# Two scratch tiles instead of four for the decay operands of the chunked DeltaNet branch

## The chip, the cores and the metric

The kernel runs on one core of a Trainium2 chip. A core has five engines with a queue of instructions each: TensorE (PE in the profile) multiplies matrices into PSUM, VectorE (DVE) and ScalarE (ACT) work elementwise, GpSimd (POOL) does small elementwise work here, and SyncE (SP) issues most of the DMAs. An engine takes its instructions strictly in the order of its queue; an instruction that has to wait for another engine, or for a DMA, holds up all that stand behind it. The metric is the time of one execution on the device in microseconds, as the median of several runs.

## The reference

One decoder layer: a half-step SwiGLU, a mixing part, another half-step SwiGLU and a final norm, over 1024 tokens and 16 meta tokens, all in float32. The mixing part has two branches, (A) a chunked gated DeltaNet with 8 heads and (B) an RWKV-7 time mixing, which are gated and added. The change lies in branch A, in these lines of the reference:

```python
g = jnp.cumsum(g, axis=-1)
kb = k * beta[..., None]
diff = g[..., :, None] - g[..., None, :]
decay = jnp.where(incl, jnp.exp(jnp.where(incl, diff, 0.0)), 0.0)
m = jnp.where(strict, jnp.einsum('bhncd,bhnsd->bhncs', kb, k) * decay, 0.0)
tinv = lax.linalg.triangular_solve(m + eye, ...)
...
attn = jnp.einsum('bhncd,bhnsd->bhncs', q, k) * decay
qg = q * jnp.exp(g)[..., None]
k_tail = k * jnp.exp(g_last[..., None] - g)[..., None]
```

So each chunk needs a decay matrix, that matrix times beta (for the matrix that is inverted), `exp(g)` along the chunk, and the decay to the chunk's end.

## The kernel before

The program has three parts: `ffn1`, `middle`, `ffn2`. Both SwiGLU parts are long runs of large matmuls. `middle` goes over two segments of the sequence (first 528 columns with the meta tokens, then 512) and, in each, over 8 heads of A with a pair of heads of B: 16 iterations in all. The iterations are pipelined by hand in `schedule()`: a regular iteration runs `merge_blocks transitions operands+ inverses+ chains gates finish new_b++ new_a++`, where a plus means the next iteration's work, and two the one after. In words:

- `new_b` and `new_a` project the normalised input (three projections each, line 262 through `proj`), with the short convolution of A at lines 1168 to 1181: `xr` holds a projection, `acc` its convolved sum over the taps (L1173), `sg` the sigmoid (L932 to L934).
- `operands` makes what the recurrences need. For A it loads the cumulated gate of one head to all partitions (`gp`, L1232), subtracts the token's own value under a mask (`E`, L1236, four chunks), takes `exp` of that (L1238) and of `gp` (`eg`, L1239), makes the tail decay `kts` (L1240, L1241), copies the chunk ends of `eg` (`egl`, L1243 on POOL), and multiplies `E` by minus beta into `E2` (L1244 on POOL). Then PE makes the products of keys with keys and queries, two chunks to a PSUM bank (`gra`, L1252), and DVE turns each bank into `UA` (times `E2`, L1255) and `attn` (times `E`, L1256). `eg` is used last, at L1314.
- `inverse_inputs` and `inverses` send the diagonal blocks of `UA` and of B's matrices (`LT`) through DRAM (`scr`) into `Ub`, and invert them by 31 steps on DVE (L1364, L1366). `merge_blocks` (PE, L1399 and after) assembles the inverses.
- `transitions` (PE, L1056: `xp`, `vp`, `mp`, `np`; DVE: `mt` L1472, `AR` L1475, `vbk` L1478) and `chains` (PE, L1526 to L1550) run the recurrences; `gates` loads a small weight (`ugr`, L1561, turned into `ug` on ACT and DVE) and makes three projections; `finish` merges.
- `new_b` begins with another small load (`upr`, L1074), turned into `upz` (L1076 on ACT, L1078 on DVE).

Scratch of one kind of size comes from one pool tag, `tmp`, with `NTMP = 8` buffers (`tmp_tile`, L847). A new tile of that tag gets a buffer when an earlier tile has had its last reader; the first writer of the new tile waits for that reader. Of these tiles `new_b` takes 13 in each iteration, `new_a` 9, `operands` 4 (`eg`, `E`, `E2`, `gp`), `gates` one (`ugr`), and `segment`, between the two segments, takes one for `urs` and eight for `uh`.

Weights are loaded on SP by `fetchw` (L223) into one of two buffers `wraw` and split by ACT and DVE (L159, L160) into two halves of `w`, one weight ahead of its use; there are two buffers of `w`.

The order of each engine's queue is fixed when the program is built: the framework takes, for each engine, the instruction that stands first in the program among those that are ready by its own estimate of times. So a tile that gets its buffer earlier by that estimate can also move its first writer to an earlier place in a queue.

Of the kernel before, what the change touches and what calls it, by code (L numbers as in the profile page):

```python
# [11 lines left out]
ALU = mybir.AluOpType  # L12

P = 128
# [12 lines left out]
FULL = 512  # L27
CB = 64
NCB = FULL // CB
CA = 128  # L30
NCA = FULL // CA
# [815 lines left out]
def tmp_tile(g, name, w=528):  # L847
    return g.st.tile([P, w], F32, name=name, tag="tmp", bufs=NTMP)


def ch3(ap, c):
    return ap.rearrange("p (a b) -> p a b", b=c)
# [341 lines left out]
def operands(g, q):  # L1194

    nc, st, V, c, j, n, off = g.nc, g.st, g.V, q.c, q.j, q.n, q.off
    meta = q.s == 0
    fs = slice(off, off + FULL)
    tmp = lambda name, w=528: tmp_tile(g, name, w)
# [16 lines left out]
    if meta:  # L1216
# [3 lines left out]
        for h in range(2):  # L1220
# [3 lines left out]
                                op=ALU.mult)  # L1224


    eg = tmp("eg")[:, :FULL]
    E = ch3(tmp("E", 512), CA)
    E2 = ch3(tmp("E2", 512), CA)
    kts = st.tile([P, NCA], F32, name="kts", tag="kts")  # L1230
    gp = tmp("gp", FULL)
    nc.sync.dma_start(gp, g.gdr[q.s][j].unsqueeze(0).to_broadcast([P, FULL]))  # L1232
    gpv = ch3(gp, CA)
    gcol = c.tk[:, :, 8 + j : 9 + j]
    for i in range(NCA):
        nc.vector.scalar_tensor_tensor(E[:, i, :], gpv[:, i, :], c.tk[:, i, 8 + j : 9 + j], g.C("mA"),  # L1236
                                       op0=ALU.subtract, op1=ALU.min)
    nc.scalar.activation(E, E, AF.Exp)  # L1238
    nc.scalar.activation(eg, gp, AF.Exp)  # L1239
    nc.vector.tensor_tensor(kts.unsqueeze(2), gpv[:, :, CA - 1 : CA], gcol, op=ALU.subtract)  # L1240
    nc.scalar.activation(kts, kts, AF.Exp)  # L1241
    egl = q.egl = st.tile([P, NCA], F32, name="egl", tag="egl", bufs=2)
    nc.gpsimd.tensor_copy(egl.unsqueeze(2), ch3(eg, CA)[:, :, CA - 1 : CA])  # L1243
    nc.gpsimd.tensor_tensor(E2, E, c.tk[:, :, 16 + j : 17 + j].to_broadcast([P, NCA, CA]), op=ALU.mult)  # L1244
    attn = q.attn = st.tile([P, NCA, CA], F32, name="attn", tag="attn", bufs=2)
    UA = q.UA = st.tile([P, NCA, CA], F32, name="UA", tag="UA", bufs=1)
    for b in range(2):
        ps = g.mx.tile([P, 512], F32, name="gra", tag="mx")
        for c2 in range(2):
            i = 2 * b + c2  # L1250
            tsl = slice(off + i * CA, off + (i + 1) * CA)
            nc.tensor.matmul(ps[:, c2 * 256 : c2 * 256 + 256], lhsT=kq[:, 0, tsl], rhs=kq[:, :, tsl],  # L1252
                             start=True, stop=True)
        pv = ps.rearrange("p (c k t) -> p c k t", c=2, k=2)
        nc.vector.tensor_tensor(UA[:, 2 * b : 2 * b + 2, :], pv[:, :, 0, :], E2[:, 2 * b : 2 * b + 2, :], op=ALU.mult)  # L1255
        nc.vector.tensor_tensor(attn[:, 2 * b : 2 * b + 2, :], pv[:, :, 1, :], E[:, 2 * b : 2 * b + 2, :], op=ALU.mult)  # L1256
    if meta:
        gm = g.mx.tile([P, 512], F32, name="gm", tag="mx")
# [326 lines left out]
def finish(g, q):  # L1585
# [17 lines left out]
    else:  # L1603
        g.mg.append(u_tile(g, yb))


ACTIONS = {"new_a": new_a, "operands": operands, "inverses": inverses, "merge_blocks": merge_blocks, "transitions": transitions,
           "chains": chains,
           "gates": gates, "finish": finish, "fill": fill}
# [86 lines left out]
```

## Time and profile before

| what | value |
|---|---|
| runs | 3085.6, 3089.95 and 3088.84 us, median 3088.84 |
| the profiled execution's own time | 3085.29 us |
| its span, first to last instruction | 3083.5 us |
| mean granted TensorE clock | 0.989 |
| PE busy over the span | 2959.3 us (96%) |
| DVE busy | 1976.2 us (64%) |
| ACT busy | 1376.7 us (45%) |
| POOL busy | 354.9 us (12%) |

The profile is one execution with a time for each instruction. In its views, `out<-in` names the tile that is written and those that are read, `x4` the number of instructions in a row, and a bracket at the end of a row tells how long the engine was idle before it and whose end released it. PE's rows are pipelined and their ends modelled, and a few records can be missing, so PE's idle time is read from its waits rather than from 100% minus its share. Buffer numbers are left out of tile names, so `E2` stands there as `E`.

### The profile page before, as it was taken

To read this page: it belongs to the slowest core of one execution; us is meant where nothing else is said; L and a number is where in the kernel's file an instruction comes from. 1 tells how busy PE (TensorE), PEld (TensorE's weight loads), DVE (VectorE), ACT (ScalarE), POOL (GpSimd) and SP (SyncE) were. 2 spreads that over 40 slices of the span, in tenths; PEclk is the share of its full clock that TensorE was granted. 3 is DMA by queue.
4 is the path that set the end of the run, shared out by engine and by line. 5 is a ranking of instruction groups with operands and counts; after the bars stand their busy time and mean duration, and the time that the engine had idled before them with its cause. 6 is when DMAs were issued, how large, how long until landed. Compare 5 with 4: busy or idle time off the path is not lost.

```text
span 3083.5 us, 61656 instructions
## 1 busy us (share of the span) xinstructions
PE 2959.3 (96%) x25498; PEld 2539.0 (82%) x25498; DVE 1976.2 (64%) x3840; ACT 1376.7 (45%) x2404; POOL 354.9 (12%) x519
## 2 busy tenths in 40 slices
PE   8999999999899999999999999999999999999998
PEld 8999998998778888788777777777777888887886
DVE  6455454346677777787867877777866655555335
ACT  5322222126555656566566655665644432222114
POOL 0222220000001000001001000010100022222000
PEclk9999999999899999999999999999999999999999
DMA  3232224234222322333332332223354232224223
GB/s 125 82 97 83 83 86 158 79 101 140 62 74 73 79 70 59 85 79 75 97 89 73 84 81 75 75 75 84 109 148 165 68 104 94 83 83 170 86 78 114
DMA packets 257593, 287.19 MB, mean 93 GB/s; under 512 B 169296, under 2 KB 175440, under 8 KB 257312
## 3 DMA queue, kind: packets, MB, share of 16 engines
q1 hardware_dynamic: 253072, 271.43, 29.4%
q0 software_dynamic: 2512, 8.65, 0.7%
q8 instruction: 201, 3.29, 0.4%
q10 hardware_dynamic: 1728, 3.16, 0.3%
q14 instruction: 80, 0.66, 0.1%
HBM read 232.70 MB, written 50.47 MB: 92 GB/s over the span
## 4 chain that ended last, share of the span: by engine, by line
PE 54%; DVE 11%; ACT 7%; issue 2%; DMA 2%; SPq 0%; DVEq 0%; POOL 0%; ACTq 0%
PE pp L262 18%; PE pg L450 12%; PE pd L262 7%; PE pwo L262 3%; DVE w L160 1%; PE pg L474 1%; PE b L1542 1%; PE cs L1003 1%; PE gra L1252 1%; DMA ugr<-in_upg 1%; PE bkt L1281 1%; DVE tb L1364 1%; DVE mt L1472 1%; DVE Xb L1366 1%; PE vp L1056 1%
## 5 line engine op out<-in xcount | busy, mean ns | idle before, releaser
L262 PE MATMUL pp<-uk,w 128*128 128x512 f32 (+2 forms) x4824 | 975.1, 347 | 15.8 <-DVE w L160 9.3
L262 PEld LDWEIGHTS pp<-uk,w 128*128 128x128 f32 x4824 | 744.7, 191 | 109.1 <-DVE w L160 13.0
L159 ACT ACTIVATE w<-wraw 128x1024 fp32r<-128x1024 f32 (+2 forms) x330 | 326.3, 989 | 712.6 <-PE pd L262 287.6
L262 PE MATMUL pd<-hd,w 128*128 128x512 f32 (+2 forms) x2640 | 495.6, 349 | 11.3 <-DVE w L160 6.7
L262 PEld LDWEIGHTS pd<-hd,w 128*128 128x128 f32 x2640 | 427.5, 189 | 78.2 <-DVE w L160 8.6
L160 DVE TENSOR_TENSOR w<-wraw,w 128x1024 fp32r<-128x1024 f32 (+2 forms) x330 | 376.1, 1140 | 90.9 <-ACT w L159 85.7
L456 DVE TENSOR_TENSOR c<-c,pg 128x520 f32<-128x520 f32 (+1 forms) x280 | 189.2, 689 | 337.3 <-PE pg L450 278.3
L450 PE MATMUL pg<-bt,w 128*128 128x256 f32 (+2 forms) x2520 | 403.9, 317 | 0.0
L450 PEld LDWEIGHTS pg<-bt,w 128*128 128x128 f32 x2520 | 361.0, 188 | 32.9 <-DVE w L160 0.2
L450 PE MATMUL pg<-b,w 128*128 128x256 f32 (+2 forms) x2160 | 348.1, 317 | 0.2 <-DVE c L456 0.2
L450 PEld LDWEIGHTS pg<-b,w 128*128 128x128 f32 x2160 | 309.8, 188 | 28.5 <-PE pg L450 0.4
L419 POOL TENSOR_TENSOR wrx<-wrx 128x512 f32<-128x512 f32 x38 | 57.2, 1505 | 755.1 <-DVE w22b L160 515.3
L1364 DVE TENSOR_TENSOR tb<-Ub,Xb 115x126 f32<-115x126 f32 (+22 forms) x496 | 124.1, 250 | 11.0 <-DMA Ub<-scr 2.7
L1366 DVE TENSOR_TENSOR Xb<-Xb,tb 115x126 f32<-115x126 f32 (+22 forms) x496 | 125.3, 253 | 8.7
L159 ACT ACTIVATE w<-wrx 128x1024 fp32r<-128x1024 f32 (+1 forms) x64 | 58.1, 908 | 156.8 <-PE pg L450 152.3
L1173 DVE SCALAR_TENSOR_TENSOR acc<-xr,pk,acc 128x528 f32<-128x528 f32 (+1 forms) x144 | 109.0, 757 | 26.4 <-ACT acc L1169 25.3
L609 DVE SCALAR_TENSOR_TENSOR h<-pd,h 128x528 f32<-128x528 f32 (+1 forms) x64 | 44.6, 698 | 115.0 <-PE pd L262 115.0
L609 DVE SCALAR_TENSOR_TENSOR hh<-pd,hh 128x512 f32<-128x512 f32 x64 | 44.2, 690 | 109.7 <-PE pd L262 106.6
L262 PE MATMUL pwo<-uk,w 128*128 128x512 f32 x384 | 101.5, 414 | 4.2 <-DVE w L160 1.9
L262 PEld LDWEIGHTS pwo<-uk,w 128*128 128x128 f32 x384 | 73.6, 197 | 22.2 <-DVE w L160 2.7
L923 ACT ACTIVATE sh<-pp,pk 128x528 f32<-128x528 f32 (+1 forms) x54 | 37.5, 694 | 98.3 <-PE pp L262 98.3
L159 ACT ACTIVATE hd<-hr 128x1040 fp32r<-128x1040 f32 (+1 forms) x44 | 45.3, 1061 | 68.6 <-DMA hr<-hid 43.7
(397 smaller groups left out, 4143.1 us busy)
## 6 DMA issues: line engine op xcount, KB each, us to landing
wraw<-in_win SPq DMA_DIRECT2D x150, 512.0 KB
wraw<-in_wgu SPq DMA_DIRECT2D x44, 512.0 KB
wrx<-in_wgu SPq DMA_DIRECT2D x44, 512.0 KB
wraw<-in_wdn SPq DMA_DIRECT2D x48, 320.0 KB
wraw<-in_wdn SPq DMA_DIRECT2D x32, 384.0 KB
hid<-c SPq DMA_DIRECT2D x44, 260.0 KB
hr<-hid SPq DMA_DIRECT2D x22, 520.0 KB
hid<-c SPq DMA_DIRECT2D x44, 256.0 KB
```

What stands on the lines that cost most here:

```text
L159: g.nc.scalar.activation(hi, src, AF.Copy)
L160: (eng or g.nc.vector).tensor_tensor(lo, src, hi.bitcast(F32), op=ALU.subtract)
L262: g.nc.tensor.matmul(ps, lhsT=l, rhs=r, start=i == 0, stop=i == n - 1)
L419: sums.tensor_tensor(a22, a21, a22, op=ALU.add)
L450: nc.tensor.matmul(ps[:, c0 : c0 + cn], lhsT=l[:, x, k, :], rhs=r[:, k, y, c0 : c0 + cn], start=i == 0, stop=i == 3 * HK - 1)
L456: nc.vector.tensor_tensor(o, x, y, op=ALU.add)
L474: nc.tensor.matmul(ps[:, c0 : c0 + cn], lhsT=l[:, x, k, :], rhs=r[:, k, y, c0 : c0 + cn], start=i == 0, stop=i == 6 * HK - 1)
L609: nc.vector.scalar_tensor_tensor(hv, pd, 0.5, hv, op0=ALU.mult, op1=ALU.add)
L923: nc.scalar.activation(sh[:, 1 : 1 + n], ps, AF.Identity, scale=g.V("mu", i))
L1173: nc.vector.scalar_tensor_tensor(acc[:, :n], xr[:, tap : tap + n], V("convw", ct * 4 + tap), acc[:, :n], op0=ALU.mult, op1=ALU.add)
L1364: nc.vector.tensor_tensor(tv, U[:, i, i + 1 :].unsqueeze(2).to_broadcast([npt, nt, ncc]), X[:, i, 0:ncc].unsqueeze(1).to_broadcast([npt, n ...
L1366: nc.vector.tensor_tensor(X[:, i + 1 :, 0:ncc], X[:, i + 1 :, 0:ncc], tv, op=ALU.add)
```

## The change

`operands` takes two `tmp` tiles, `E` and `gp`, where it took four. `eg` becomes a name for `gp`: the exponential is taken in place, once the tail decay `kts` has read `gp`'s last columns, and so `kts` is made ahead of it. `E2` is gone: in place of one multiplication on POOL and a two-chunk product per bank, DVE makes `UA` by a three-operand product per chunk, the PSUM part times minus beta (one value for each partition) times `E`. All else stays.

```diff
-    eg = tmp("eg")[:, :FULL]
     E = ch3(tmp("E", 512), CA)
-    E2 = ch3(tmp("E2", 512), CA)
     kts = st.tile([P, NCA], F32, name="kts", tag="kts")
     gp = tmp("gp", FULL)
     nc.sync.dma_start(gp, g.gdr[q.s][j].unsqueeze(0).to_broadcast([P, FULL]))
...
     nc.scalar.activation(E, E, AF.Exp)
+    nc.vector.tensor_tensor(kts.unsqueeze(2), gpv[:, :, CA - 1 : CA], gcol, op=ALU.subtract)
+    eg = gp
     nc.scalar.activation(eg, gp, AF.Exp)
-    nc.vector.tensor_tensor(kts.unsqueeze(2), gpv[:, :, CA - 1 : CA], gcol, op=ALU.subtract)
     nc.scalar.activation(kts, kts, AF.Exp)
     egl = q.egl = st.tile([P, NCA], F32, name="egl", tag="egl", bufs=2)
     nc.gpsimd.tensor_copy(egl.unsqueeze(2), ch3(eg, CA)[:, :, CA - 1 : CA])
-    nc.gpsimd.tensor_tensor(E2, E, c.tk[:, :, 16 + j : 17 + j].to_broadcast([P, NCA, CA]), op=ALU.mult)
...
         pv = ps.rearrange("p (c k t) -> p c k t", c=2, k=2)
-        nc.vector.tensor_tensor(UA[:, 2 * b : 2 * b + 2, :], pv[:, :, 0, :], E2[:, 2 * b : 2 * b + 2, :], op=ALU.mult)
+        for i in (2 * b, 2 * b + 1):
+            nc.vector.scalar_tensor_tensor(UA[:, i, :], pv[:, i % 2, 0, :], c.tk[:, i, 16 + j : 17 + j], E[:, i, :],
+                                           op0=ALU.mult, op1=ALU.mult)
         nc.vector.tensor_tensor(attn[:, 2 * b : 2 * b + 2, :], pv[:, :, 1, :], E[:, 2 * b : 2 * b + 2, :], op=ALU.mult)
```

## Prediction, made before the changed kernel was run

> **What bounds the kernel now.** I read the page's busy shares first, then the middle part, the only one with an instruction of the change, by its busy times and by who PE waited for.
>
> ```profile
> span 3083.5 us, 61656 instructions
> PE 2959.3 (96%) x25498; PEld 2539.0 (82%) x25498; DVE 1976.2 (64%) x3840; ACT 1376.7 (45%) x2404; POOL 354.9 (12%) x519
> 800.00:2330.00 1530.00, 1449.85 (x16443) 1193.15 (x16441) 1164.82 (x2762) 885.68 (x1735) 120.51 (x298) 0.99 0.31 83
> PE np L1056 <- DVE AR L1475: 14.1, 15, 2.3
> PE pp L262 <- DVE w L160: 9.3, 11, 2.8
> ...
> PE vbp L1056 <- DVE vB L924: 4.8, 1, 4.8
> ```
>
> The third row gives, for 1530 us around the sixteen iterations, busy us of PE, weight loads, DVE, ACT and POOL: PE works 1450 of them. The last rows give us in total, times and the longest. PE bounds the middle too; all that can be won are the 80 us it is idle, and the largest wait has 14.1. None of these waits names `E`, `eg`, `UA` or POOL. So removed work is worth little by itself; what counts is whether two more free buffers shorten a wait.
>
> **What the removed and added instructions cost.**
>
> ```profile
> L1244 POOL TENSOR_TENSOR E<-E,tk x16: 1044/1049/1804, 812.7 to 2214.1; 128x512 f32<-128x512 f32 x16
> L1255 DVE TENSOR_TENSOR UA<-gra,E 128x256 f32<-128x256 f32 x32 | 13.4, 418 | 11.7 <-PE gra L1252 9.9 <-issue 1.6
> L1534 DVE SCALAR_TENSOR_TENSOR SA<-SA,egl,p 128x128 f32<-128x128 f32 x64 | 22.1, 345 | 23.8 <-PE p L1533 23.1
> ...
> L1236 DVE SCALAR_TENSOR_TENSOR E<-gp,tk,ck x64: 332/343/351, 810.2 to 2211.7; 128x128 f32<-128x128 f32 x64
> L1239 ACT ACTIVATE eg<-gp x16: 612/616/636, 809.4 to 2211.2; 128x512 f32<-128x512 f32 x16
> ```
>
> *POOL.* Sixteen `E2` products go, 1.05 us each. Their result isn't waited for: the rows of one iteration below have `E2` done at 1083.96 and `UA` at 1097.21, after PE's `gra`. Gain 0; below nothing it can't go, as POOL has fewer instructions and none is added.
>
> *DVE.* Two `UA` products of 418 ns become four three-operand ones on half the columns. The nearest row is L1534: same operation and shape, PSUM and a per-partition factor included, 345 ns. So 4 x 345 - 2 x 418 = 544 ns more an iteration, 8.7 us for sixteen. The Trainium skill speaks against such a split: "VectorE: DVE Perf Modes", section "The TRN2 errata — SBUF-src ops pay a fixed extra latency per instruction", says that each instruction pays a fixed latency however small it is, with (N+151)/0.96 ns for a float32 product. By that, an estimate, 256 columns take 424 ns, near the row's 418, and 128 take 291, so the split would cost 4 x 291 - 2 x 424 = 316 ns, 16 x 0.316 = 5.1 us in all in place of 8.7. The row of the operation itself is dearer, and the sum goes by the row.
>
> What hides it is DVE's idle time. In the first segment it comes before `UA`, `em` and `SB`:
>
> ```profile
> 1095.60 0.28 DVE L1500 COPY rhm<-bm 16x128 f32<-16x128 f32 x1
> 1097.21 0.42 DVE L1255 TENSOR_TENSOR UA<-gra,E 128x256 f32<-128x256 f32 x1 [1.32 <-PE gra L1252]
> 1097.55 0.41 DVE L1256 TENSOR_TENSOR attn<-gra,E 128x256 f32<-128x256 f32 x1
> 1098.00 0.42 DVE L1255 TENSOR_TENSOR UA<-gra,E 128x256 f32<-128x256 f32 x1
> 1098.34 0.41 DVE L1256 TENSOR_TENSOR attn<-gra,E 128x256 f32<-128x256 f32 x1
> 1099.59 0.58 DVE L1509 TENSOR_SCALAR SB<-bm,elm 64x64 f32<-64x64 f32 x2 [0.27 <-PE bm L1507]
> ...
> 2053.04 0.41 DVE L1255 TENSOR_TENSOR UA<-gra,E 128x256 f32<-128x256 f32 x1
> 2054.55 0.27 DVE L1524 TENSOR_TENSOR rhA<-Va,p 128x128 f32<-128x128 f32 x1
> 2057.45 0.69 DVE L1308 TENSOR_TENSOR ktl<-ktp,kts 128x512 f32<-128x512 f32 x1 [2.62 <-PE ktp L1307]
> ```
>
> The first product starts when PE's `gra` lets it, so the delay begins behind it and reaches `em` and `SB`, behind which PE has projections (`pp`) in its queue. In the second segment (last three rows) `UA` stands in a run without idle time; `SBs` and `rhA` behind it, which the chains wait for, come half a us later, and the 2.62 us before `ktl` take up the rest. I let 1 us of the 8.7 reach PE; bounds 0 and 8.7.
>
> *ACT.* `eg` in place must wait for the four `E` subtractions and `kts`. ACT has the same 616 ns to do; of `eg`'s readers, `egl` on POOL is used by the chains alone, and L1314 stands behind `UA` in the program, so neither is near. 0. If `eg` reaches the head of ACT's queue too soon, the weight splits and `E`'s own exponential behind it wait for the subtractions: 4 x 0.343 us, so 1.4 us at most in an iteration in which it happens.
>
> **What moves: three DMAs.** The ring gives `gp`, `ugr` and `upr` a buffer two allocations earlier: reckoned from the code, `gp` today gets that of the second `xr` (last tap L1173), `ugr` and `upr` those of the second `acc` and `sg` (L1181). With `eg` and `E2` gone the ones freed before them serve: the first `acc` and `sg`, and the third `xr`. One iteration:
>
> ```profile
> 1066.05 0.33 SPq L1232 DMA_DIRECT2D gp<-gdr  x1
> 1076.67 5.38 SPq L223 DMA_DIRECT2D wraw<-in_win  x2
> 1082.11 0.42 SPq L1561 DMA_DIRECT2D ugr<-in_upg  x1
> 1082.58 0.43 SPq L1074 DMA_DIRECT2D upr<-in_upwa  x1
> ...
> 1069.94 0.71 DVE L1181 TENSOR_TENSOR kq<-acc,sg 128x528 f32<-128x528 f32 x1 [3.34 <-ACT sg L1024]
> 1073.74 0.76 DVE L1173 SCALAR_TENSOR_TENSOR acc<-xr,pk,acc 128x528 f32<-128x528 f32 x1
> 1076.56 0.70 DVE L1181 TENSOR_TENSOR kq<-acc,sg 128x528 f32<-128x528 f32 x1
> ...
> 1082.91 1.05 POOL L1244 TENSOR_TENSOR E<-E,tk 128x512 f32<-128x512 f32 x1 [3.49 <-ACT E L1238]
> 1085.54 0.31 ACT L159 ACTIVATE ug<-ugr 128x128 fp32r<-128x128 f32 x1 [0.48 <-DMA ugr<-in_upg]
> 1085.88 0.29 DVE L160 TENSOR_TENSOR ug<-ugr,ug 128x128 fp32r<-128x128 f32 x1 [4.18 <-ACT ug L159]
> 1087.41 0.42 ACT L1076 ACTIVATE upz<-upr 128x256 fp32r<-128x256 f32 x1 [1.36 <-DMA upr<-in_upwa]
> 1087.87 0.59 DVE L1078 TENSOR_TENSOR upz<-upr,upz 64x128 fp32r<-64x128 f32 x2 [1.39 <-ACT upz L1076]
> 1088.46 1.73 DVE L1472 TENSOR_TENSOR mt<-mp,ck 64x256 f32<-64x256 f32 x4
> 1090.78 0.41 PE L1056 MATMUL np<-xv,BKt 64*64 64x64 f32 x7 [2.27 <-DVE AR L1475]
> ```
>
> The buffers behind `ugr` and `upr` come free at 1077.3 today (L1181's end), after the first of two weight loads that wait on SP for their own buffers (the row of 1076.67 holds both, to 1082.05), and both DMAs stand behind the second. Freed at 1070.7 and 1074.5, they can stand ahead of the first: issued some 8 to 11 us earlier and landed by 1080 (from issue to ACT's first reader it is 1085.54 - 1082.11 = 3.4 us for `ugr` and 1087.41 - 1082.58 = 4.8 for `upr`). Then DVE doesn't stand idle 4.18 and 1.39 us for them; `mt` starts when `mp` is there, `AR` follows, and `np`, which needs the PSUM buffer that `AR` reads out, comes sooner.
>
> How much of that PE sees: DVE's idle time before `ug` and `upz` is
>
> ```profile
> DVE ug L160 <- ACT ug L159: 34.6, 9, 5.9
> 2048.62 0.41 PE L1056 MATMUL np<-xv,BKt 64*64 64x64 f32 x6 [0.48 <-DVE AR L1475]
> SPq L1561 <- DVE acc L1177: 27.1, 3, 9.2
> ```
>
> 34.6 us in nine iterations, but most of it lies beside PE's own `mp` matmuls. Where DVE isn't held up (the row at 2048.62) `np` still waits 0.48 us. Of its 14.1 us in 15 waits, 15 x 0.48 = 7.2 are that floor; 6.9 can go. I take 5, as some of the longer ones may have another cause; bounds 0 and 6.9. In the last iterations `ugr` already stands ahead of the weight loads and waits there for its buffer (27.1 us in three); an earlier one frees SP, but the next load waits for `w` anyway: 0. Each DMA moved ahead of a weight load takes 0.4 us of SP, while that load isn't issued for 10 us after `gp`: 0. If SP came to wait there for `ugr`'s buffer longer than for the load's own, the load would be late; that is part of what the range must hold. `gp` (256 KB) lands earlier than it is used in either order. Between the segments the nine tiles `urs` and `uh` want eight buffers as before, so the last load still waits: 0.
>
> **Sum.** -5 + 1 = -4 us on the profiled execution: 3085.3 to 3081.3. That execution lies 3.5 us below the runs' median of 3088.84, so the median becomes 3084.8, -0.13%. A measurement of this kernel tells a change of about 0.2% from none: 6.2 us, faster below 3082.7, slower above 3095.0.
>
> **Rivals.**
>
> *More than the one wait.* Each queue's order is made anew with the earlier buffers, and some 35 us of idle DVE go before the stage that feeds `mt`, `LT` and the weight splits. Then the waits for `w` (9.3 us) and the single one for `vB` (4.8) can shrink as well: with 6.9 and at most these 14, -10 to -20; half of it, with the 6.9, is -14, 3074.8. For it: these are single long waits (2.8 and 4.8 us), which a new order needn't repeat. Against: none of them names a tile of the ring.
>
> *No effect that can be measured.* `ugr` and `upr` stay behind the weight loads, or the DVE stall turns up before another instruction, while the split hides: 0 to +1, 3089. For it: most of the 34.6 us costs PE nothing now.
>
> *Slower: the split on the path.* In the second segment `UA` and `attn` read out the two `gra` banks within a run of DVE instructions without a gap; if PE waits for what stands behind them in each iteration, in both segments, all 8.7 us come in and nothing is won: 3097.5. It decides once the DVE run from `upz` to `rhA` has no idle time and PE no projection left beside it. For it: that run at 2053. Against: in the first segment DVE is idle 1.32 us right before.
>
> **How the numbers follow.** Forecast 0.35, by itself 3082 to 3089 (from 6.9 won and nothing lost to 5 won and 5 lost); of it 0.07 falls under 3082.7 and 0.28 within 0.2%. More than the one wait 0.33, faster. No effect 0.14, within. Slower 0.18. So faster 0.40, same 0.42, slower 0.18. The range, 3073 to 3097, takes in the first rival's -14 with 2 us to spare, and the third's to half a us from its full price; beyond lie a further gain and a stall that an earlier `ugr` puts into the convolution, 0.2 together.
>
> **What would show it.** Right: `ugr` and `upr` issued on SP before the two weight loads that follow `gp`; no idle time of some 4 us on DVE before `ug`; `np` waiting about 0.5 us in each iteration, some 7 to 9 in total; four `UA` products near 345 ns; POOL's L1244 gone and nobody later for it. Wrong: `np` waits stay at 14 us; or PE's new longest waits name `SBs`, `rhA` or `em`, or `sg` and `acc` of the convolution behind a DVE that waits for `ugr`; or a gain or a loss sits in waits that name none of these, which would be the new order of the queues and not this step.

## The result and the profile after

The changed kernel takes 3072.07 us, the median of six runs (3070.59 to 3076.21); the kernel before, in six runs, 3088.9. The ratio is 0.995 with a 95% interval of 0.994 to 0.996: faster by half a per cent, clear of the 0.2% that can be told from no change. Forecast were 3084.8 us, -0.13%, with a chance of 0.42 for no change that can be told and 0.40 for faster, and the range ended at 3073, 0.9 us above the median that came. Nearest is the first rival, "more than the one wait", at 3074.8, but in the number only: of the two waits that it named, the one for `w` fell by 2.1 us and the one for `vB` by 0.1. One execution of fold_only below took 4905.54 us at a granted clock of 0.65, and its median is that of the other four.

Page of the changed kernel, span and busy times, then the middle part (span, then busy us and counts of PE, weight loads, DVE, ACT and POOL, the granted clock and the DMA's share and GB/s):

```profile
span 3069.3 us, 61679 instructions
PE 2950.7 (96%) x25498; PEld 2535.0 (83%) x25498; DVE 1977.9 (64%) x3872; ACT 1376.0 (45%) x2404; POOL 325.2 (11%) x503
800.00:2330.00 1530.00, 1450.07 (x16471) 1195.28 (x16470) 1174.88 (x2806) 890.16 (x1743) 91.03 (x282) 0.98 0.32 85
```

The span is 14.2 us shorter. PE's busy time is 8.6 us less for the same 25498 matmuls, so only 5.6 of the 14.2 us come from stretches in which PE's rows show it idle. POOL has 16 instructions and 29.7 us less, of which the products were 19.0 (a mean of 1.19 us each; the 1.05 of the prediction is their median); the rest lies in small copies. DVE does no less than before. Who PE waited for in the middle, in us in total, times, longest:

```profile
PE xp L1056 <- ACT at L1460: 12.1, 13, 1.3
PE np L1056 <- DVE AR L1475: 8.9, 15, 1.6
PE pp L262 <- DVE w L160: 7.2, 5, 3.0
...
PE vbp L1056 <- DVE vB L924: 4.7, 1, 4.7
...
PE tkp L979 <- DVE c L965: 3.9, 1, 3.9
...
PE vbm L1118 <- ACT Vs L1115: 1.7, 6, 0.7
```

Two of these rows in the kernel before:

```profile
PE vbm L1118 <- ACT Vs L1115: 5.8, 7, 1.0
...
PE xp L1056 <- ACT at L1460: 4.2, 8, 1.0
```

`np` fell from 14.1 to 8.9 us, 5.2 less: the forecast had taken 5. But `vbm` fell too, by 4.1 us, and the waits for `w` by 2.1, which the forecast had left to a rival. Other waits are new or longer, above all `xp` for `at` and a single one for `c`, between the segments.

DVE's own waits in the middle, and one regular iteration of the first segment (SP's queue, then DVE's; a row has start, duration, engine, line, operation, tiles, and in brackets the idle time before it and its releaser):

```profile
DVE mt L1472 <- PE mp L1056: 32.7, 15, 4.0
...
DVE ug L160 <- ACT ug L159: 19.5, 13, 2.7
```

```profile
1062.58 0.38 SPq L1230 DMA_DIRECT2D gp<-gdr  x1
1070.25 0.33 SPq L223 DMA_DIRECT2D wraw<-in_win  x1
1070.63 1.40 SPq L1561 DMA_DIRECT2D ugr<-in_upg  x1
1072.13 0.38 SPq L1074 DMA_DIRECT2D upr<-in_upwa  x1
```

```profile
1077.78 0.29 DVE L160 TENSOR_TENSOR ug<-ugr,ug 128x128 fp32r<-128x128 f32 x1 [0.77 <-ACT ug L159]
1078.51 0.28 DVE L1566 TENSOR_TENSOR ug<-ugr,ug 32x128 fp32r<-32x128 f32 x1 [0.43 <-ACT ug L1564]
1078.81 0.59 DVE L1078 TENSOR_TENSOR upz<-upr,upz 64x128 fp32r<-64x128 f32 x2
1083.43 1.73 DVE L1472 TENSOR_TENSOR mt<-mp,ck 64x256 f32<-64x256 f32 x4 [4.03 <-PE mp L1056]
```

Read this against the same iteration of before. `ugr` is issued 8 us after `gp` where it was 16 us, and behind one weight load where it was behind two. DVE stood idle 4.18 us for `ug` and 1.39 for `upz`, and then began `mt` at once; now it has `ug` and `upz` done early and stands 4.03 us in front of `mt` because PE hasn't finished `mp`. Idle time of DVE that nobody waited for has taken the place of idle time that held PE up.

Where the 14.2 us were won: both traces hold all 4824 `pp` matmuls of L262, so the start of the same one can be compared. Before lags behind after by 1.7 us at the 1057th (961.4 us in the trace of after, just ahead of the third `gp`), by 11.8 at the 2689th (1414.6, near the end of the first segment's regular iterations), by only 4.8 at the 3553rd (1739.1, after the switch of segments), by 9.8 at the 3937th (1900.8, the twelfth iteration), and by 13.4 at the last `pwo` (2377.3). So 1.7 us come from the start, 10.1 from the first segment, 7.0 are given back at the switch, 5.0 come from one stretch of the second segment, and 4.4 from what follows.

The first segment is the clean part: five regular iterations, third to seventh. The stretch from the issue of the third's `gp` to that of the eighth's, before and after:

```profile
968.30:1454.90 486.60, 463.14 (x5626) 396.15 (x5626) 368.46 (x895) 282.11 (x574) 36.85 (x112) 1.00 0.29 75
```

```profile
967.60:1444.80 477.20, 460.20 (x5630) 398.01 (x5628) 369.44 (x906) 282.50 (x577) 29.64 (x110) 1.00 0.29 76
```

97.3 us an iteration became 95.4. PE's time outside its busy time went from 486.6 - 463.1 = 23.5 us to 17.0; DVE had the same work in less time. All experiments are read by this stretch, each in its one profiled execution.

### The profile page after: what moved, and what is told of

It reads as the page before. It is cut to its first block, busy times and chain, and to the rows that moved or that the text cites. A ratio compares the mean times of both kernels' runs of the same rounds, so it can differ in the third digit from the quotient of the medians.

```text
span 3069.3 us, 61679 instructions
## 1 busy us (share of the span) xinstructions
PE 2950.7 (96%) x25498; PEld 2535.0 (83%) x25498; DVE 1977.9 (64%) x3872; ACT 1376.0 (45%) x2404; POOL 325.2 (11%) x503
## 3 DMA queue, kind: packets, MB, share of 16 engines
q1 hardware_dynamic: 253072, 271.43, 29.7%
## 5 line engine op out<-in xcount | busy, mean ns | idle before, releaser
L262 PE MATMUL pp<-uk,w 128*128 128x512 f32 (+2 forms) x4824 | 968.5, 347 | 11.2 <-DVE w L160 7.2
L262 PEld LDWEIGHTS pp<-uk,w 128*128 128x128 f32 x4824 | 748.7, 191 | 105.2 <-DVE w L160 9.0
L262 PE MATMUL pd<-hd,w 128*128 128x512 f32 (+2 forms) x2640 | 495.8, 350 | 10.1 <-DVE w L160 5.8
L262 PEld LDWEIGHTS pd<-hd,w 128*128 128x128 f32 x2640 | 427.6, 189 | 77.2 <-DVE w L160 7.6
L262 PE MATMUL pwo<-uk,w 128*128 128x512 f32 x384 | 100.6, 413 | 3.3 <-DVE w L160 1.9
L262 PEld LDWEIGHTS pwo<-uk,w 128*128 128x128 f32 x384 | 73.4, 196 | 20.7 <-DVE w L160 2.5
```

What stands on the lines that cost most here:

```text
L262: g.nc.tensor.matmul(ps, lhsT=l, rhs=r, start=i == 0, stop=i == n - 1)
```

## The experiments

Theories at the start: **ring** (the change frees scratch buffers, so `ugr` and `upr` come earlier: the prediction's), **fold** (POOL's product itself held something up), **in-place** (the new place of the exponentials on ACT counts), and **order** or **luck** (each edit makes the queues' order anew, and the new one happened to be better). After the first four runs a fifth was formed, **place**: what costs time is that `ugr` and `upr` stand late on SP, however they came there.

All of them, with the distance from `gp`'s issue to `ugr`'s, mean of the five regular iterations, and the length of the five:

| kernel | what it is | ugr after gp, us | five iterations, us | median, us | ratio to before, 95% |
|---|---|---|---|---|---|
| before | | 16.1 | 486.6 | 3088.9 | |
| after | | 9.3 | 477.2 | 3072.07 | 0.995 (0.994 to 0.996) |
| eg_inplace | in-place exponential alone | 10.9 | 477.1 | 3074.86 | 0.996 (0.9948 to 0.9973) |
| fold_only | folded product alone | 9.8 | 475.8 | 3074.53 | 0.9955 (0.9941 to 0.9969) |
| split_old_ring | four tiles, split product | 10.7 | 474.1 | 3076.22 | 0.9957 (0.9945 to 0.997) |
| e2_in_ua | two tiles, no split | 10.7 | 478.3 | 3078.17 | 0.9963 (0.9949 to 0.9977) |
| swap_attn | before, two statements swapped | 9.1 | 472.2 | 3072.89 | 0.9949 (0.9937 to 0.9962) |
| e2_dve | before, E2 on DVE | 16.2 | 490.5 | 3089.76 | 1.0002 (0.9993 to 1.0011) |
| after_late_up | after, loads held | 16.7 | 489.0 | 3087.55 | 0.9997 (0.9988 to 1.0006) |
| up_pool | before, loads on POOL | 18.9 | 502.0 | 3107.1 | 1.0058 (1.0045 to 1.0072) |
| up_sub_pool | before, their subtractions on POOL | 16.2 | 477.3 | 3076.04 | 0.9955 (0.9942 to 0.9967) |
| swap_fold | fold_only and the swap | 9.5 | 474.3 | 3085.32 | 0.9989 (0.9979 to 0.9999) |
| after_swap | after and the swap | 8.7 | 475.5 | 3069.67 | 0.9942 (0.9928 to 0.9955) |
| after_sub_pool | after, subtractions on POOL | 9.5 | 477.8 | 3071.39 | 0.9945 (0.9931 to 0.9958) |

The ratios go by executions of before that were taken together with each kernel: their medians are 3087.29 us for the first four experiments, 3089.06 for the next four in the order of the table (swap_attn to up_pool) and 3088.28 for the last four.

### One edit at a time

**eg_inplace**, against before:

```diff
-    eg = tmp("eg")[:, :FULL]
...
-    nc.scalar.activation(eg, gp, AF.Exp)
     nc.vector.tensor_tensor(kts.unsqueeze(2), gpv[:, :, CA - 1 : CA], gcol, op=ALU.subtract)
+    eg = gp
+    nc.scalar.activation(eg, gp, AF.Exp)
```

> The in-place decay alone: kts first, then exp written over gp; E2 stays on POOL and UA stays two products of two chunks. One scratch tile less than before. Theory ring (the gain comes from scratch buffers that are free earlier, and each tile given back brings part of it): between before and the full change, about 3080, PE waiting for AR about 9 to 12 us. Theory in-place (what counts is that kts and the two exponentials stand in another order on ACT, the freed buffer nothing): the whole gain, 3072. Theory fold (the gain comes from the POOL product that is gone): no gain, 3089.

**fold_only**, against before:

```diff
-    E2 = ch3(tmp("E2", 512), CA)
...
-    nc.gpsimd.tensor_tensor(E2, E, c.tk[:, :, 16 + j : 17 + j].to_broadcast([P, NCA, CA]), op=ALU.mult)
...
-        nc.vector.tensor_tensor(UA[:, 2 * b : 2 * b + 2, :], pv[:, :, 0, :], E2[:, 2 * b : 2 * b + 2, :], op=ALU.mult)
+        for i in (2 * b, 2 * b + 1):
+            nc.vector.scalar_tensor_tensor(UA[:, i, :], pv[:, i % 2, 0, :], c.tk[:, i, 16 + j : 17 + j], E[:, i, :],
+                                           op0=ALU.mult, op1=ALU.mult)
```

> The folded product alone: E2 and its POOL product are gone, UA is made by four three-operand products; eg keeps its own scratch tile and its place. One scratch tile less than before. Theory ring: about 3080, at most 3089 if the split costs its full 8.7 us. Theory in-place: 3089, or slower by up to 8.7 us for the split. Theory fold: the whole gain, 3072.

**split_old_ring**, against before (`E2` keeps its tile and its last reader, but only four columns of it are written):

```diff
-    nc.gpsimd.tensor_tensor(E2, E, c.tk[:, :, 16 + j : 17 + j].to_broadcast([P, NCA, CA]), op=ALU.mult)
+    nc.gpsimd.tensor_copy(E2[:, :, 0:1], c.tk[:, :, 16 + j : 17 + j])
...
-        nc.vector.tensor_tensor(UA[:, 2 * b : 2 * b + 2, :], pv[:, :, 0, :], E2[:, 2 * b : 2 * b + 2, :], op=ALU.mult)
+        for i in (2 * b, 2 * b + 1):
+            nc.vector.scalar_tensor_tensor(UA[:, i, :], pv[:, i % 2, 0, :], E2[:, i, 0:1], E[:, i, :],
+                                           op0=ALU.mult, op1=ALU.mult)
```

> The four three-operand products with the scratch tiles of before: E2 is still allotted, written on POOL (with the four beta columns only, 128x4) and read by the same products, so that four tiles are taken and given back at the old places. Theory ring: nothing is freed, so no gain: 3089 with the split hidden, up to 3098 with all of it on the path; PE waits for AR as before, about 14 us. Theory order (any edit makes every queue's order anew, and the gain is the luck of that new order, whatever the ring): a change of some 10 us either way, and if ugr and upr come to stand ahead of the weight loads without the ring's help, a gain of 5 to 15 us.

**e2_in_ua**, against the changed kernel:

```diff
+    nc.gpsimd.tensor_tensor(UA, E, c.tk[:, :, 16 + j : 17 + j].to_broadcast([P, NCA, CA]), op=ALU.mult)
...
-        for i in (2 * b, 2 * b + 1):
-            nc.vector.scalar_tensor_tensor(UA[:, i, :], pv[:, i % 2, 0, :], c.tk[:, i, 16 + j : 17 + j], E[:, i, :],
-                                           op0=ALU.mult, op1=ALU.mult)
+        nc.vector.tensor_tensor(UA[:, 2 * b : 2 * b + 2, :], pv[:, :, 0, :], UA[:, 2 * b : 2 * b + 2, :], op=ALU.mult)
```

> Two scratch tiles as in the full change, without the split: POOL writes E times minus beta into UA itself, and DVE multiplies UA in place, two products of 418 ns per iteration. POOL now waits for the last reader of the UA before. Theory ring: at least the full change's gain, 3072, and 1 us less where the split was hidden, up to 8.7 us less (3063) where it stood on the path. Theory fold: no gain, 3089, as POOL's product is back. Theory order: anywhere within 10 us of the full change.

All four are faster than before, with intervals that overlap: 3074.5 to 3078.2 us. Each of the two edits alone brings nearly the whole gain, where ring had said about 3080 for each, so they don't add up, and neither edit is needed for it. Against in-place stand fold_only and split_old_ring, which gain without the in-place exponential. Against ring stands split_old_ring, which gives back no tile and gains as much (3076.22, where ring said 3089 or more). What the four share is SP's queue; of split_old_ring, in the fourth iteration:

```profile
1068.36 0.33 SPq L1232 DMA_DIRECT2D gp<-gdr  x1
1078.15 0.33 SPq L223 DMA_DIRECT2D wraw<-in_win  x1
1079.01 0.33 SPq L1563 DMA_DIRECT2D ugr<-in_upg  x1
1079.39 0.42 SPq L1074 DMA_DIRECT2D upr<-in_upwa  x1
```

With as many tiles as before, `ugr` goes out behind the first weight load instead of the second, some 11 us after `gp` instead of 16. A freed buffer isn't needed for that; a new order is. That left two theories, place and luck.

### Is it the place of the two loads?

**swap_attn**, against before:

```diff
-        nc.vector.tensor_tensor(UA[:, 2 * b : 2 * b + 2, :], pv[:, :, 0, :], E2[:, 2 * b : 2 * b + 2, :], op=ALU.mult)
         nc.vector.tensor_tensor(attn[:, 2 * b : 2 * b + 2, :], pv[:, :, 1, :], E[:, 2 * b : 2 * b + 2, :], op=ALU.mult)
+        nc.vector.tensor_tensor(UA[:, 2 * b : 2 * b + 2, :], pv[:, :, 0, :], E2[:, 2 * b : 2 * b + 2, :], op=ALU.mult)
```

> The kernel before with two statements swapped: attn's product stands ahead of UA's. Same instructions, same scratch tiles, nothing removed; only the queues' order is new, and by it ugr and upr stand ahead of the second weight load after gp (segment one) or ahead of the first (segment two). Theory place (what costs time is that ugr and upr stand behind two weight loads on SP; anything that brings them forward wins it): 3072 to 3078, iterations of the first segment 95 to 95.5 us in place of 97.6, ugr issued about 11 us after gp or earlier in place of 16. Theory ring, theory fold, theory in-place: no gain, 3087 to 3089.

The same instructions and the same tiles as before, in another order: 3072.89 us, the whole gain. SP's rows in the fourth iteration:

```profile
1062.30 1.11 SPq L1232 DMA_DIRECT2D gp<-gdr  x1
1071.86 0.33 SPq L1561 DMA_DIRECT2D ugr<-in_upg  x1
1072.48 0.33 SPq L1074 DMA_DIRECT2D upr<-in_upwa  x1
```

**e2_dve**, against before:

```diff
-    nc.gpsimd.tensor_tensor(E2, E, c.tk[:, :, 16 + j : 17 + j].to_broadcast([P, NCA, CA]), op=ALU.mult)
+    nc.vector.tensor_tensor(E2, E, c.tk[:, :, 16 + j : 17 + j].to_broadcast([P, NCA, CA]), op=ALU.mult)
```

> The kernel before with the product E2 on DVE in place of POOL: POOL's work is gone, DVE has one 128x512 product more in each iteration (about 0.6 to 1.1 us), and SP's order keeps ugr and upr behind two weight loads in the first segment. Theory place: no gain, 3086 to 3092, first-segment iterations 97 us or more. Theory fold in its other form (POOL's product itself held something up): a gain of 5 us or more. Theory luck: no view, as the orders stay those of before.

POOL is relieved as in the change (DVE has the product in its place), `ugr` stays at 16.2 us, and nothing is won: 1.0002 (0.9993 to 1.0011). Together with eg_inplace, e2_in_ua and swap_attn, which gain though POOL's product stays, that ends fold.

**after_late_up**, against the changed kernel (the same two lines stand ahead of `upr`'s load):

```diff
-    egl = q.egl = st.tile([P, NCA], F32, name="egl", tag="egl", bufs=2)
+    egl = g.egl_now = q.egl = st.tile([P, NCA], F32, name="egl", tag="egl", bufs=2)
...
     raw = tmp_tile(g, "ugr", 512).rearrange("p (a m) -> p a m", m=P)
+    if getattr(g, "egl_now", None) is not None:
+        nc.gpsimd.tensor_copy(raw[:, 0, 0:1], g.egl_now[:, 0:1])
     nc.sync.dma_start(raw[:, 0:2, :], g.a["upg"][j])
```

> The changed kernel with one dependency added: a one-column copy on POOL from egl into the tile that ugr or upr is loaded into, so that these two loads wait until egl is there, 16 to 17 us after gp. Most iterations of the first segment then have them behind two weight loads on SP again. Theory place: most of the gain is lost, 3080 to 3088, first-segment iterations back at 97 us and PE's waits for AR longer by 4 us or more in total. Theory luck or theory in-place: 3072 with 5 us either way, and iterations of 95 us though ugr is late.

With both edits in place, holding the two loads takes the whole gain back: 3087.55, 0.9997 of before, and five iterations of 489.0 us. SP and DVE in the fourth iteration:

```profile
1066.67 0.36 SPq L1232 DMA_DIRECT2D gp<-gdr  x1
1074.92 1.52 SPq L223 DMA_DIRECT2D wraw<-in_win  x2
1083.08 0.33 SPq L1565 DMA_DIRECT2D ugr<-in_upg  x1
```

```profile
1086.29 0.29 DVE L160 TENSOR_TENSOR ug<-ugr,ug 128x128 fp32r<-128x128 f32 x1 [5.53 <-ACT ug L159]
```

The picture of before is back: two weight loads ahead of `ugr`, and DVE idle for 5.53 us.

**up_pool**, against before:

```diff
-    nc.sync.dma_start(raw[:, 0:2, :], g.a["upwa"][j])
+    nc.gpsimd.dma_start(raw[:, 0:2, :], g.a["upwa"][j])
...
-    nc.sync.dma_start(raw[:, 0:2, :], g.a["upg"][j])
+    nc.gpsimd.dma_start(raw[:, 0:2, :], g.a["upg"][j])
```

> The kernel before with ugr and upr issued from POOL's queue in place of SP's, so that they wait for their scratch buffer alone and for no weight load; the rest of the code is that of before. Theory place: the buffer is free some 11 us after gp, so ugr is there in time and the iterations of the first segment take about 95.5 us, the ninth to twelfth iteration about 87: 3074 to 3079. Theory luck (the gain is a sum of many small shifts of the new orders, not this place): within 5 us of before, 3082 to 3092, as PE's order stays nearest to that of before.

Both theories missed: 3107.1 us, slower than before. The loads got away from SP's weight loads and behind something worse on POOL:

```profile
1084.37 1.04 POOL L1244 TENSOR_TENSOR E<-E,tk 128x512 f32<-128x512 f32 x1 [5.07 <-ACT E L1238]
1085.36 0.58 POOL L1561 DMA_DIRECT2D ugr<-in_upg  x1
1085.94 0.54 POOL L1074 DMA_DIRECT2D upr<-in_upwa  x1
```

They stand behind `E2`, which waits for the exponential: `ugr` now goes out 19 us after `gp`. As a test of place it served in part, from the other side: later by 2.8 us than before on the mean, and five iterations longer by 15.4 us. Of these, 11.4 stand in PE's busy time (474.55 us against 463.14), at a granted clock of 0.97 in the stretch where before has 1.00, so this isn't the price of the wait alone.

### What carries the delay to PE?

**up_sub_pool**, against before:

```diff
-    split(g, raw[:, 0, :], up[:, 0, :], up[:, 1, :])
+    split(g, raw[:, 0, :], up[:, 0, :], up[:, 1, :], eng=nc.gpsimd)
...
-    nc.vector.tensor_tensor(u3, raw[64:96, 1, :], u3.bitcast(F32), op=ALU.subtract)
+    nc.gpsimd.tensor_tensor(u3, raw[64:96, 1, :], u3.bitcast(F32), op=ALU.subtract)
...
-        nc.vector.tensor_tensor(up[sl, 2 + i, :], raw[sl, i, :], up[sl, i, :].bitcast(F32), op=ALU.subtract)
+        nc.gpsimd.tensor_tensor(up[sl, 2 + i, :], raw[sl, i, :], up[sl, i, :].bitcast(F32), op=ALU.subtract)
```

> The kernel before with the three small subtractions of ug and upz on POOL in place of DVE (128x128, 32x128 and two of 64x128); ugr and upr still stand behind two weight loads on SP in the first segment. Theory stall (the late loads cost time because DVE, in order, stands idle before ug and upz and all its later work slips): the first-segment iterations come down to 95 to 96 us though ugr is still issued some 16 us after gp, and the time to 3073 to 3079. Theory weight (what costs is the other order on SP itself, the weight loads or ACT's copies of the late tiles): iterations stay at 97 us, 3080 to 3090.

Here the loads are as late as before (16.2 us, behind two weight loads) and only their first readers on DVE are gone from it. The fourth iteration, SP, POOL and DVE:

```profile
1063.52 0.33 SPq L1232 DMA_DIRECT2D gp<-gdr  x1
1074.10 5.38 SPq L223 DMA_DIRECT2D wraw<-in_win  x2
1079.53 0.42 SPq L1561 DMA_DIRECT2D ugr<-in_upg  x1
```

```profile
1083.36 0.46 POOL L160 TENSOR_TENSOR ug<-ugr,ug 128x128 fp32r<-128x128 f32 x1 [1.98 <-ACT ug L159]
1083.90 0.45 POOL L1566 TENSOR_TENSOR ug<-ugr,ug 32x128 fp32r<-32x128 f32 x1
```

```profile
1083.65 1.73 DVE L1472 TENSOR_TENSOR mt<-mp,ck 64x256 f32<-64x256 f32 x4 [4.53 <-PE mp L1056]
```

`ug` is made at 1083.4, late, but on an engine that can wait; `mt` no longer stands behind it. The five iterations take 477.3 us, as after the change, and the time is 3076.04. So in the first segment the loads' lateness costs time through one thing: DVE, in order, stands idle in front of `ug` and `upz`, and `mt`, `AR`, `LT` and all that follows slips. PE's waits in the five iterations, before and then in this kernel:

```profile
PE np L1056 <- DVE AR L1475: 6.1, 5, 2.3
PE vbm L1118 <- ACT Vs L1115: 5.0, 5, 1.0
```

```profile
PE np L1056 <- DVE AR L1475: 1.0, 4, 0.3
PE vbm L1118 <- ACT Vs L1115: 1.0, 5, 0.2
```

`np` gives 5.1 us and `vbm`, many instructions later in the same iteration, another 4.0; together 9.1 us, and the stretch is 9.3 us shorter. In the second segment this kernel's order is also another one, with `ugr` at 9.6 us or less, so its total doesn't speak for the stall alone; the five iterations do.

How long DVE is idle is not the measure. In the five iterations eg_inplace (first three rows) and e2_dve (last two) have the same idle time in front of `ug`, and one is fast and the other isn't:

```profile
DVE ug L160 <- ACT ug L159: 13.6, 5, 3.6
DVE mt L1472 <- PE mp L1056: 4.0, 5, 0.8
PE np L1056 <- DVE AR L1475: 1.4, 5, 0.5
```

```profile
DVE ug L160 <- ACT ug L159: 13.4, 5, 3.9
PE np L1056 <- DVE AR L1475: 7.7, 5, 2.2
```

What tells them apart is the second row: in eg_inplace DVE is through with `ug` and `upz` in time to wait for PE's `mp`, in e2_dve it isn't. It is the same in all fourteen traces. In the ten kernels whose five iterations take 472 to 478 us, `mt` waits for `mp` in all five, whether by 4.0 us in total or by 30.4 (after_sub_pool), and the waits of `np` and `vbm` together are 2.0 to 3.9 us. In the four with 486 to 502 us it never waits, or once (after_late_up), and the two are 11.1 to 15.6.

### Can more be won?

**swap_fold** is fold_only with the swap of swap_attn, **after_swap** the changed kernel with it, **after_sub_pool** the changed kernel with the edits of up_sub_pool:

```diff
+        nc.vector.tensor_tensor(attn[:, 2 * b : 2 * b + 2, :], pv[:, :, 1, :], E[:, 2 * b : 2 * b + 2, :], op=ALU.mult)
         for i in (2 * b, 2 * b + 1):
...
-        nc.vector.tensor_tensor(attn[:, 2 * b : 2 * b + 2, :], pv[:, :, 1, :], E[:, 2 * b : 2 * b + 2, :], op=ALU.mult)
```

> The kernel before with attn's product ahead of UA's and the folded product: no E2, no POOL product, four three-operand products; eg keeps its own tile. If the in-place decay costs what PE's longer waits for at hint (some 8 us of waits, of which perhaps half reach the end), this one is the fastest: 3066 to 3071. If those waits only took the place of others, 3072 to 3076, as the swap alone.

> The changed kernel with attn's product ahead of UA's, so the in-place decay and the fold with another order again. If ugr comes early already, the swap has nothing left to win: 3069 to 3076, PE waiting for at some 15 us. If the swap had a gain of its own beside the place of ugr and upr, 3060 to 3067.

> The changed kernel with the three small subtractions of ug and upz on POOL. Theory stall: some of DVE's idle time before ug is left in the changed kernel, so up to 3 us more are won, 3066 to 3073. Theory weight: 3072 with 3 us either way.

after_swap and after_sub_pool lie within the interval of the changed kernel; no version here is shown to beat it. In after_sub_pool DVE no longer waits for `ug` at all, and the five iterations stay at 477.8 us: what was left of that wait after the change cost nothing.

swap_fold missed: it keeps the short iterations of the first segment (474.3 us) and loses about 10 us elsewhere. Its twelfth iteration takes 98.6 us between two issues of `gp`, where fold_only's takes 86.6. The same stretch, swap_fold and then fold_only:

```profile
1843.00:1930.00 87.00, 79.25 (x860) 62.35 (x859) 66.19 (x160) 45.01 (x87) 4.52 (x11) 0.96 0.28 73
```

```profile
1843.00:1930.00 87.00, 83.45 (x940) 66.68 (x939) 71.34 (x167) 53.12 (x103) 6.22 (x15) 1.00 0.31 82
```

PE starts 80 fewer matmuls in the same 87 us, is idle 4.2 us longer, and has a granted clock of 0.96. `ugr` is not late there (10.6 us after `gp`), so this is another effect of an order. From 1584 to 2120 us PE waits 5.7 us for weights (`w`) in swap_fold and 0.7 in fold_only, so the weights may be what is late; it was not tried.

## Why the prediction was right and wrong

**Right.** The place: that the queues mattered and not the removed work, that `ugr` and `upr` are the instructions to watch and would be issued earlier (8 us in the iteration shown and 6.8 on the mean of five, where 8 to 11 were foretold), that DVE's idle time before `ug` was the wait that shrinks, and `np` with it, by 5 us to some 7 to 9 in total (5.2, to 8.9). POOL's product at 0: nothing is won by taking it off POOL in e2_dve, and eg_inplace and swap_attn gain with it in place.

**The split.** The four products measured

```profile
L1254 DVE SCALAR_TENSOR_TENSOR UA<-gra,tk,E 128x128 f32<-128x128 f32 x64 | 19.4, 345 | 11.6 <-PE gra L1250 11.6
```

345 ns each, as row L1534 had said. These rows overlap, so DVE's busy time for `UA` grew from 13.4 to 19.4 us, 6.0 more, where the sum had 8.7. The estimate from the Trainium skill's page "VectorE: DVE Perf Modes", section "The TRN2 errata — SBUF-src ops pay a fixed extra latency per instruction", was 291 by its figure for a two-operand addition, which the page measured on 512 and 2048 columns. The measurement decides. That its cost hides was right as far as can be seen: e2_in_ua, without the split, isn't faster than the changed kernel.

**Wrong: the size of the stall.** The step that failed is "How much of that PE sees". It counted `np` alone, because `np` was the wait whose chain could be followed back to `ug`, and set 5 us against 34.6 us of idle DVE. In the five regular iterations the time won is 9.4 us; the two waits are now

```profile
PE np L1056 <- DVE AR L1475: 1.7, 5, 0.5
...
PE vbm L1118 <- ACT Vs L1115: 1.0, 5, 0.2
```

Of the 9.4 us `np` has 6.1 - 1.7 = 4.4, and `vbm`, further down the same iteration, 5.0 - 1.0 = 4.0; up_sub_pool shows that it hangs on the same stall. The other waits moved both ways: `iv` for `XA` fell by 1.8 us and `pp` for `w` by 0.9, `xp` for `at` grew by 2.9 and `bm` for `yb` by 2.3. By the prediction's own list of signs, a gain in waits that it didn't name would be the new order and not this step; up_sub_pool shows that `vbm` is this step. The argument held against the first rival, that none of its waits names a tile of the ring, was no argument: an engine that is late passes its lateness on to whatever it makes next, and the wait then bears that tile's name. Nor does the waits' list carry all: of the 9.4 us, PE's time outside busy shrank by 6.5, and its busy time for the same matmuls by 2.9. Short stalls that stand in the modelled ends of PE's rows would look like that; no run shows it.

**Wrong: the means.** "The ring gives gp, ugr and upr a buffer two allocations earlier" was taken as what moves the loads. split_old_ring and swap_attn move them as far without a freed buffer. What is shown is that the loads' place, as long as DVE reads them, decides the first segment, and that several edits, a swap of two statements among them, lead to the better order; whether in the changed kernel itself the freed buffers or the new order did it, stays open. The loads also don't stand "ahead of the first" weight load there, as foretold, but behind one or, in some iterations, still two, which go out earlier themselves.

**Wrong: ACT at 0.** PE's waits of `xp` for `at` grew from 4.2 to 12.1 us. In the five iterations they are 2.9 us after the change, 2.2 in eg_inplace and 2.1 in e2_in_ua, which have the exponential in place, but also 1.3 in swap_attn, which hasn't, and 0.7 or less in before, fold_only and split_old_ring. In the first four of these kernels ACT takes, in the fourth iteration, `E`'s own exponential (0.61 us) ahead of the copies to `at` that `xp` waits for: after the change they start at 1076.32 and 1078.69 us, with copies of `ug` and `upz` in between. In the other three it stands behind them: in before it starts at 1082.15 and they at 1081.36. So it is again the order of a queue, which the in-place exponential can bring but isn't needed for; no run tested that alone. What these waits cost at the end can't be told: swap_attn without the in-place decay and after_swap with it have overlapping intervals.

**Not foreseen.** 7.0 us were given back at the switch of segments. The new wait of `tkp` for `c`, 3.9 us, isn't shown to be the reason: the stretch from the eighth `gp` to the ninth takes 136.6 us before and 141.8 after, and 140.6 in eg_inplace, where that wait is 0.9 us. In this stretch PE is busy 131.1 us after the change and 127.9 before, at a granted clock of 0.95 against 1.00; no run took it apart, and it stays open. And the twelfth iteration takes 92.9 us before and 86.8 after. Before has `ugr` 15.6 us after `gp` there, so the same stall fits, but the thirteenth has it at 16.1 us and takes 88.5, and swap_fold shows that this stretch can be long for another reason too; it stays a likely cause and not a shown one.

## What to carry to other kernels

When an in-order engine stands idle for a small operand, look at what it does next: if its next large instruction then has to wait for the bottleneck engine, the idle time costs nothing, and if it starts at once, all that stands behind it in that iteration is late, not only the one wait that can be followed back. Moving the operand's readers to an engine with time to spare (the subtractions of `ug` and `upz` to POOL here, five iterations from 486.6 to 477.3 us) tests it in one run. Where a compiler or framework makes the queues' order, repeat a change with a neutral edit beside it before believing its reason: swapping two statements gave all of this change's gain. And a load's place in its queue is worth looking at first: with `ugr` 9 to 11 us after `gp` the iterations took 94.4 to 95.7 us without a trend, and, as long as its readers stayed on DVE, 97 to 98 at 16 to 17 us and 100.4 at 19.

## What was not expected of the hardware

Sending two small loads from POOL's queue to avoid SP's made the kernel slower (3107.1 us): POOL took 0.58 and 0.54 us to issue them, and, in order like SP, held them behind a wait of 5.07 us for the exponential of `E`. An engine that is 12% busy isn't an engine that is free when it is needed.
